# Attention of a two-layer hybrid block: order of the transposes and value products on TensorE, and another spread of the softmax normalisers

## The chip, the cores and the metric

The kernel runs on one core of a Trainium2 chip. Its time is the device time of one execution in microseconds. The core's engines are TensorE (PE in the profile; its weight loads are a row of their own, PEld), VectorE (DVE), ScalarE (ACT), GpSimd (POOL) and SyncE (SP), which issues most of the DMAs. Each engine works through its own queue in order.

## The reference

Two layers of a block over 256 context tokens and 1024 latent tokens of width 1024. Each layer normalises and modulates its input, projects it once, and feeds three groups: a bidirectional SSD, attention, and a convolution module; each is gated, the results are concatenated, projected and added. Only the attention concerns the change. It has 8 heads of 64 in two key/value groups of four heads, and looks at all context keys and a band of latent keys, with a sink logit per head:

```python
def window_attention(q, k, v, kc, vc, sink):
    ...
    s_win = einsum('bnqgrd,bnkgd->bngrqk', qb, kw) * scale      # three blocks of 128 keys, |qpos - kpos| <= 128
    s_ctx = einsum('bnqgrd,btgd->bngrqt', qb, kc) * scale       # 256 context keys
    p = softmax(concatenate([sink_col, s_ctx, s_win]))
    out = (einsum('bngrqt,btgd->bnqgrd', p[..., 1:1 + n_ctx], vc)
           + einsum('bngrqk,bnkgd->bnqgrd', p[..., 1 + n_ctx:], vw))
```

In the first layer the two blocks of context queries attend to the context too; in the last layer there are no context queries.

## The kernel before

Each layer runs three sections in turn: the SSD section, the attention section (att_section, line 965), and the output section. Matmuls of the projections are done in three parts (high by high, low by high, high by low, gemm1, line 464) into tiles named pj.

att_section first makes keys, values and rotated queries, then runs core(n) (line 1024) for each block n of 128 queries: ten calls in layer 0 (two of them context blocks), eight in layer 1. Between the calls it lets the generator rest() (line 1226) go on: the remaining gate projections, the second normalisation of the convolution module and its projection. The loop is at lines 1268 to 1275; each core is traced within high_priority(AHEAD) with AHEAD = 4000, two steps of rest() follow each call.

The code is not in the order of execution. The framework simulates the engines, and gives each engine's next place to the instruction of the highest priority that is ready by that simulation; priority is the place in the program, moved forward by high_priority. The resulting order of each engine's queue is fixed before the program runs. A tile with bufs=2 has two buffers; its third user waits until the first is released.

core(n) has nk key blocks in the list kb: two context blocks, the block itself, and its neighbours where they exist. So nk is 2 for a context block, 4 for the first and the last latent block, 5 for the rest. It works in two halves (for r0 in (0, 2), line 1053) of four heads each:

- Scores of four heads (tiles s5 and s4) with masks added by a matmul with the negated identity; row minimum on VectorE (lines 1064, 1076), Exp with the row sum on ScalarE (lines 1079, 1081) into a tile p of queries by keys. p has six buffers, four of them used by one half.
- For each key block i (line 1083): four transposes (line 1086), one a head, into one PSUM tile pt (two buffers); a copy into the SBUF tile ptt (two buffers), on ScalarE for even i and on VectorE for odd i (lines 1088 to 1091); and two value products (line 1093), one a key/value group. Each has 64 columns of stationary values, 256 columns moving, and adds into its half of the 128 partitions of the PSUM tile op (named o in the rows), which has one buffer.

Behind both halves the normalisers are made: sums with the sink term, and the reciprocal (lines 1095 to 1100), a column per head with a query per partition. They are spread along the free axis by eight matmuls (line 1105) into the tile rb (a buffer of pt): the column, broadcast to 64 columns, as the stationary operand, and the identity moving. A copy to rs on ScalarE (line 1107) and a product on VectorE (line 1108) write the result over the queries, which releases op for the next core.

All matmuls made by the helper mm carry its line, L96, and are told apart by tile names.

Of the kernel before, what the change touches and what calls it, by code (L numbers as in the profile page):

```python
# [2 lines left out]

# [7 lines left out]
F32 = mybir.dt.float32  # L11
# [3 lines left out]
AF = mybir.ActivationFunctionType  # L15
# [4 lines left out]
P = 128  # L20
# [41 lines left out]
RX0 = 6  # L62
NH = 3
NAG = (2, 4)
SEP = (4, 2, 2, 2, 9)


def build(tc, A, out, stop=None, dbg=None):
    nc = tc.nc
# [19 lines left out]
    def f32(ap):  # L89
        return ap.bitcast(F32)  # L90
# [2 lines left out]
        return ap.bitcast(F32R)  # L93

    def mm(o, l, r, start=True, stop=True):
        nc.tensor.matmul(o, l, r, start=start, stop=stop)  # L96

    def spread(o, col):

# [2 lines left out]
    def flat(ap):  # L102
        return ap.rearrange("p a b -> p (a b)")


    ident = cp.tile([P, P], F32, name="ident")
# [155 lines left out]
    with ExitStack() as st:  # L262
# [3 lines left out]
        def tr():  # L266
            return ipp.tile([P, 512], F32, tag="tr", name="tr", bufs=3)
# [22 lines left out]
        pt = tr()  # L290
# [250 lines left out]
    def ssd_section(l, last, early):  # L541
        v1 = vec1[l]
        gblocks = LATB if last else ALLB
        with ExitStack() as st:
# [248 lines left out]
            def gate_gemm(r):  # L793

                w = load_w(l, ((C_AG + r * 64, 64), (C_AG + 256 + r * 64, 64)))

                def use(off, n, ps):
                    t = sp.tile([P, 512], F32, tag="sz", name="ag", bufs=3)[:, 0:n]
                    nc.scalar.activation(out=t, in_=ps, func=AF.Copy)
                    nc.scalar.dma_start(out=agd[l][:, r, off:off + n], in_=t)  # L800
                for blk in gblocks:
                    gemm(l, w, (blk,), use)
# [147 lines left out]
            for i in range(4):  # L950
# [6 lines left out]
                if i == 1:  # L957
                    bc_group(1)
            for r in range(NAG[l]):
                gate_gemm(r)  # L960
# [4 lines left out]
    def att_section(l, last):  # L965
# [5 lines left out]
        with ExitStack() as st:  # L971
# [7 lines left out]
            vtok = sa.tile([P, NCH, P], F32, name="vtok")  # L979
# [42 lines left out]
            sp = pool(f"atc{l}", 1, None, st)  # L1022

            def core(n):
                if n < 2:
                    kb = [0, 1]
                else:
                    kb = [0, 1] + ([n - 1] if n > 2 else []) + [n] + ([n + 1] if n < NCH - 1 else [])
                mpos = [i for i, b in enumerate(kb) if b >= 2 and b != n]
                runs = []  # L1030
                for i, b in enumerate(kb):
                    if runs and runs[-1][0] + runs[-1][2] == b and i < 4:
                        runs[-1][2] += 1
                    else:
                        runs.append([b, i, 1])
                nk = len(kb)
                nb_ = slice(n * P, (n + 1) * P)
                Q = []
                for g in range(2):
                    a, b = slice(g * 64, g * 64 + 64), slice(64 - g * 64, 128 - g * 64)  # L1040
                    t = sp.tile([P, 4, P], F32R, tag="Q", name="Q", bufs=3)
                    nc.scalar.activation(out=t[a], in_=qt[a, :, nb_], func=AF.Copy)
                    nc.vector.tensor_tensor(out=t[b], in0=qt[a, :, nb_], in1=f32(t[a]), op=ALU.subtract)
                    Q.append(t)
                sums = sp.tile([P, 5, 8], F32, tag="sums", name="sums", bufs=2)
                nm, sm_, ns = (sums[:, i, :] for i in range(3))
                op = pp.tile([P, 512], F32, tag="o", name="o")

                def scores(o, g, r, b, cnt, fin, first=True):
                    for ki, K in enumerate((KH[g], KL[g])):  # L1050
                        mm(o, Q[g][:, r, :], K[:, b * P:(b + cnt) * P], start=(first and ki == 0), stop=(fin and ki == 1))

                for r0 in (0, 2):
                    heads = [(g, r) for g in range(2) for r in (r0, r0 + 1)]
                    pr = []

                    if nk > 4:
                        s5 = pp.tile([P, 4, P], F32, tag="s5", name="s5")

                        mm(s5, nident, mask_gt.unsqueeze(1).to_broadcast([P, 4, P]), stop=False)  # L1060
                        for q, (g, r) in enumerate(heads):
                            scores(s5[:, q, :], g, r, kb[4], 1, q == 3, first=False)
                        m5 = sp.tile([P, 4], F32, tag="m5", name="m5", bufs=2)
                        nc.vector.tensor_reduce(out=m5, in_=s5, axis=mybir.AxisListType.X, op=ALU.min)
                    for q, (g, r) in enumerate(heads):
                        s4 = pp.tile([P, 4, P], F32, tag="s4", name="s4", bufs=2)
                        for b, i, cnt in runs:
                            if i < 4:
                                scores(flat(s4[:, i:i + cnt, :]), g, r, b, cnt, not any(x in range(i, i + cnt) for x in mpos))
                        for i in mpos:  # L1070
                            if i < 4:
                                mm(s4[:, i, :], nident, mask_lt if kb[i] < n else mask_gt, start=False, stop=True)
                        s = flat(s4[:, 0:min(nk, 4), :])
                        j = g * 4 + r
                        mx = sp.tile([P, 1], F32, tag="mx", name="mx", bufs=3)
                        nc.vector.tensor_reduce(out=mx, in_=s, axis=mybir.AxisListType.X, op=ALU.min)  # L1076
                        nc.vector.scalar_tensor_tensor(out=nm[:, j:j + 1], in0=mx, scalar=nsink[l][:, j:j + 1], in1=m5[:, q:q + 1] if nk > 4 else mx, op0=ALU.min, op1=ALU.min)  # L1077
                        p = sp.tile([P, 5, P], F32, tag="p", name="p", bufs=6)
                        nc.scalar.activation(out=flat(p[:, 0:min(nk, 4), :]), in_=s, func=AF.Exp, scale=-1.0, bias=nm[:, j:j + 1], accum_out=sums[:, 3, j:j + 1])  # L1079
                        if nk > 4:  # L1080
                            nc.scalar.activation(out=p[:, 4, :], in_=s5[:, q, :], func=AF.Exp, scale=-1.0, bias=nm[:, j:j + 1], accum_out=sums[:, 4, j:j + 1])
                        pr.append(p)
                    for i, b in enumerate(kb):
                        pt = pp.tile([P, 512], F32, tag="pt", name="pt", bufs=2)
                        for q in range(4):
                            nc.tensor.transpose(pt[:, q * P:(q + 1) * P], pr[q][:, i, :], ident)  # L1086
                        ptt = sp.tile([P, 512], F32, tag="ptt", name="ptt", bufs=2)
                        if i % 2:
                            nc.vector.tensor_copy(out=ptt, in_=pt)
                        else:  # L1090
                            nc.scalar.activation(out=ptt, in_=pt, func=AF.Copy)
                        for g in range(2):
                            mm(op[g * 64:(g + 1) * 64, r0 * P:(r0 + 2) * P], vtok[:, b, g * 64:(g + 1) * 64], ptt[:, g * 256:(g + 1) * 256], start=(i == 0), stop=(i == nk - 1))

                nc.vector.tensor_tensor(out=ns, in0=nm, in1=nsink[l], op=ALU.subtract)
                nc.scalar.activation(out=ns, in_=ns, func=AF.Exp)
                nc.vector.tensor_tensor(out=sm_, in0=sums[:, 3, :], in1=ns, op=ALU.add)
                if nk > 4:
                    nc.vector.tensor_tensor(out=sm_, in0=sums[:, 4, :], in1=sm_, op=ALU.add)
                nc.vector.reciprocal(out=sm_, in_=sm_)  # L1100
                rb = pp.tile([P, 512], F32, tag="pt", name="rb", bufs=2)
                for r in range(4):
                    for g in range(2):
                        j = g * 4 + r
                        mm(rb[g * 64:(g + 1) * 64, r * P:(r + 1) * P], sm_[:, j:j + 1].to_broadcast([P, 64]), ident)
                rs = sp.tile([P, 512], F32, tag="ptt", name="rs", bufs=2)
                nc.scalar.activation(out=rs, in_=rb, func=AF.Copy)
                nc.vector.tensor_tensor(out=qt[:, :, nb_], in0=op.rearrange("p (a b) -> p a b", b=P), in1=rs.rearrange("p (a b) -> p a b", b=P), op=ALU.mult)
# [117 lines left out]
            def rest():  # L1226

                def units():
                    rs = list(range(NAG[l], 4))
                    for J in range(8):  # L1230
# [6 lines left out]
                for off, n in qblocks:  # L1237
                    us = sp.tile([P, 4, 512], F32, tag="us", name="us")[:, :, 0:n]
                    for _, k in zip(conv_norm(off, n, us), SEP):
                        for _ in range(k):  # L1240
# [229 lines left out]
```

## Time and profile before

| | us |
|---|---|
| median of 3 runs | 2414.48 (2412.67 to 2416.03) |
| profiled execution, its own time | 2409.47 |
| span of the profiled execution | 2407.7 |
| TensorE busy | 2307.0 (96%), 13453 matmuls |
| VectorE busy | 1533.2 (64%) |
| GpSimd busy | 1085.7 (45%) |
| ScalarE busy | 979.0 (41%), 2123 instructions |

The attention cores of layer 0 run from about 690 to 1040 us of the span, those of layer 1 from about 1875 to 2203. Matmuls overlap: the length of one in the trace goes on past the start of the next, so their distance from start to start tells what they cost. A value product is two entries (passes) in the trace, as is a matmul of the normaliser spread; a transpose and a projection matmul are one. The timeline merges entries of one kind that follow each other, with their number behind the x.

### The profile page before, as it was taken

To read this page: it belongs to the slowest core of one execution; us is meant where nothing else is said; L and a number is where in the kernel's file an instruction comes from. 1 tells how busy PE (TensorE), PEld (TensorE's weight loads), DVE (VectorE), ACT (ScalarE), POOL (GpSimd) and SP (SyncE) were. 2 spreads that over 40 slices of the span, in tenths; PEclk is the share of its full clock that TensorE was granted. 3 is DMA by queue.
4 is the path that set the end of the run, shared out by engine and by line. 5 is a ranking of instruction groups with operands and counts; after the bars stand their busy time and mean duration, and the time that the engine had idled before them with its cause. 6 is when DMAs were issued, how large, how long until landed. Compare 5 with 4: busy or idle time off the path is not lost.

```text
span 2407.7 us, 37133 instructions
## 1 busy us (share of the span) xinstructions
PE 2307.0 (96%) x13453; PEld 1817.5 (75%) x13453; DVE 1533.2 (64%) x2738; ACT 979.0 (41%) x2123; POOL 1085.7 (45%) x1249
## 2 busy tenths in 40 slices
PE   6999999999999999999999999999999999999998
PEld 3787678777877776776888788768768676776798
DVE  4679899941276855865354679979423864865634
ACT  6543243422235454444243443343322355463433
POOL 3237663764453222343233337667575531332333
PEclk8999999999999999999999999999999999999999
DMA  7412212233133112248465311111212312235663
GB/s 225 154 58 87 87 49 64 85 100 111 36 90 105 62 38 70 80 141 264 136 185 168 92 40 45 41 41 43 78 54 62 106 48 67 80 97 171 197 179 107
DMA packets 324248, 237.07 MB, mean 98 GB/s; under 512 B 56066, under 2 KB 280546, under 8 KB 324064
## 3 DMA queue, kind: packets, MB, share of 16 engines
q1 hardware_dynamic: 280832, 193.28, 27.2%
q10 hardware_dynamic: 42336, 41.06, 5.5%
q8 instruction: 106, 1.74, 0.3%
q0 software_dynamic: 896, 0.35, 0.1%
q14 instruction: 78, 0.64, 0.1%
HBM read 181.63 MB, written 53.00 MB: 97 GB/s over the span
## 4 chain that ended last, share of the span: by engine, by line
PE 77%; DVE 9%; DMA 5%; POOL 3%; issue 2%; ACT 2%; SPq 1%; ACTq 0%; DVEq 0%; POOLq 0%
PE pj L96 53%; PE sm L96 6%; PE s L96 4%; PE o L96 3%; PE pt L1086 3%; PE po L96 2%; DVE us L508 2%; DMA raw<-oT 1%; PE pc L96 1%; PE pm L96 1%; DMA wm<-w_mod 1%; POOL ex L893 1%; PE rb L96 1%; DVE acc L596 1%; PE sm L912 1%
## 5 line engine op out<-in xcount | busy, mean ns | idle before, releaser
L96 PE MATMUL pj<-hh,wh 128*128 128x512 f32 (+1 forms) x1840 | 692.7, 377 | 7.8 <-ACT wh L416 2.3
L96 PE MATMUL pj<-hl,wh 128*128 128x512 f32 (+1 forms) x1840 | 686.5, 373 | 1.7 <-POOL hl L199 1.7
L96 PE MATMUL pj<-hh,wl 128*128 128x512 f32 (+1 forms) x1840 | 686.4, 373 | 1.7 <-POOL wl L418 1.6
L418 POOL TENSOR_TENSOR wl<-wr,wh 128x512 fp32r<-128x512 f32 x268 | 362.1, 1354 | 516.8 <-ACT wh L416 482.1
L96 PEld LDWEIGHTS pj<-hh,wh 128*128 128x128 f32 x1840 | 350.0, 190 | 70.7 <-issue 6.8
L96 PEld LDWEIGHTS pj<-hh,wl 128*128 128x128 f32 x1840 | 349.5, 190 | 61.3 <-issue 5.0
L96 PEld LDWEIGHTS pj<-hl,wh 128*128 128x128 f32 x1840 | 350.2, 190 | 59.3 <-issue 5.7
L416 ACT ACTIVATE wh<-wr 128x512 fp32r<-128x512 f32 x344 | 215.6, 630 | 365.5 <-PE pj L96 280.2
L508 DVE SCALAR_TENSOR_TENSOR ua<-gl,vec,ua 128x512 f32<-128x512 f32 (+1 forms) x435 | 303.5, 698 | 12.3 <-ACT ua L506 5.7
L596 DVE SCALAR_TENSOR_TENSOR acc<-raw,vec,acc 128x514 f32<-128x514 f32 (+2 forms) x280 | 191.0, 695 | 21.9 <-ACT acc L593 20.3
L96 PE MATMUL pj<-ho,wh 128*128 128x256 f32 (+1 forms) x896 | 180.3, 300 | 1.0 <-ACT wh L416 1.0
L96 PE MATMUL pj<-hx,wh 128*128 128x512 f32 x512 | 163.7, 400 | 6.9 <-DVE hx L500 2.9
L96 PEld LDWEIGHTS pj<-ho,wh 128*128 128x128 f32 x896 | 145.2, 193 | 6.4 <-ACT wh L416 1.2
L893 POOL TENSOR_TENSOR ex<-ex,eb 64x256 f32<-64x256 f32 x144 | 115.5, 802 | 59.4 <-ACT eb L891 52.4
L933 POOL TENSOR_TENSOR xs<-xk,ws 128x256 f32<-128x256 f32 x144 | 90.7, 641 | 112.0 <-PE sm L96 96.8
L1079 ACT ACTIVATE p<-s,sums 128x512 f32<-128x512 f32 (+1 forms) x144 | 95.5, 663 | 107.7 <-DVE sums L1077 69.4
L1076 DVE TENSOR_REDUCE mx<-s 128x1 f32<-128x512 f32 (+1 forms) x144 | 92.4, 654 | 72.0 <-PE s L96 71.6
L96 PE MATMUL pj<-ho,wl 128*128 128x256 f32 (+1 forms) x448 | 134.6, 301 | 1.1 <-POOL wl L418 0.8
L508 DVE SCALAR_TENSOR_TENSOR us<-gl,vec,us 128x512 f32<-128x512 f32 (+1 forms) x150 | 130.3, 869 | 6.8 <-ACT us L506 4.3
L96 PEld LDWEIGHTS pj<-hx,wh 128*128 128x128 f32 x512 | 97.8, 192 | 30.6 <-DVE hx L500 4.7
L907 POOL TENSOR_TENSOR yp<-yp,ye 128x256 f32<-128x256 f32 x136 | 104.3, 783 | 26.6 <-DVE ye L906 26.1
L1086 PE MATMUL pt<-ident,p 128*128 128x128 f32 x640 | 108.5, 283 | 7.2 <-ACT p L1079 6.5
(325 smaller groups left out, 3951.6 us busy)
## 6 DMA issues: line engine op xcount, KB each, us to landing
wr<-w_in SPq DMA_DIRECT2D x160, 256.0 KB
wr<-w_out SPq DMA_DIRECT2D x114, 256.0 KB
wm<-w_mod SPq DMA_DIRECT2D x64, 256.0 KB
raw<-oT ACTq DMA_DIRECT2D x64, 256.0 KB
wr<-w_out SPq DMA_DIRECT2D x76, 128.0 KB
yT<-yT ACTq DMA_DIRECT2D x72, 128.0 KB
wm<-w_mod SPq DMA_DIRECT2D x16, 512.0 KB
wr<-w_in SPq DMA_DIRECT2D x64, 128.0 KB
```

What stands on the lines that cost most here:

```text
L96: nc.tensor.matmul(o, l, r, start=start, stop=stop)
L416: nc.scalar.activation(out=hi, in_=raw, func=AF.Copy)
L418: low_eng[0].tensor_tensor(out=lo, in0=raw, in1=f32(hi), op=ALU.subtract)
L508: nc.vector.scalar_tensor_tensor(out=u if t == 30 else acc, in0=g[:, t:t + n], scalar=vec2[l][:, t, j:j + 1], in1=acc, op0=ALU.mult, op1=A ...
L596: nc.vector.scalar_tensor_tensor(out=acc, in0=raw[:, i0 + t:i0 + t + n], scalar=v1[:, cw:cw + 1], in1=acc, op0=ALU.mult, op1=ALU.add)
L893: nc.gpsimd.tensor_tensor(out=e[q, :, q], in0=e[q, :, q], in1=eb[q], op=ALU.add)
L907: nc.gpsimd.tensor_tensor(out=y, in0=y, in1=ye, op=ALU.add)
L912: nc.tensor.matmul(ps[:, jj * P:(jj + 1) * P], y[:, jj * P:(jj + 1) * P], ident, start=(jj == 0), stop=False, is_transpose=True)
L933: nc.gpsimd.tensor_tensor(out=h3(xs), in0=xc(c), in1=hb(ws3, c, d), op=ALU.mult)
L1076: nc.vector.tensor_reduce(out=mx, in_=s, axis=mybir.AxisListType.X, op=ALU.min)
L1079: nc.scalar.activation(out=flat(p[:, 0:min(nk, 4), :]), in_=s, func=AF.Exp, scale=-1.0, bias=nm[:, j:j + 1], accum_out=sums[:, 3, j:j + 1])
L1086: nc.tensor.transpose(pt[:, q * P:(q + 1) * P], pr[q][:, i, :], ident)
```

## The change

Inside a half, the loop over key blocks is split. The transposes and the copy of one block become the function turn(i). Blocks 0 and 1 are turned first. Then, for each pair of blocks, the next two blocks are turned, with a priority 40 places further forward, and behind them the value products of the pair are traced within issue_after, which makes each TensorE instruction in it stand behind the last transpose in TensorE's queue. Where a pair has no further block to turn, the last transpose is that of an earlier turn.

The normalisers are first copied by ScalarE into a tile nx (which takes one of the six p buffers): 128 queries by four blocks of 128, each of the two halves of a block holding one head's normaliser 64 times. Four whole transposes of these blocks into rb take the place of the eight matmuls.

```diff
+TURN = 40
 ...
+        return nc.tensor.matmul(o, l, r, start=start, stop=stop)
+
+    def after(ins):
+        return tc.issue_after(ins[0].ins) if ins else nullcontext()
 ...
-                    for i, b in enumerate(kb):
+                    ptts, last_t = [], []
+
+                    def turn(i):
                         pt = pp.tile([P, 512], F32, tag="pt", name="pt", bufs=2)
                         for q in range(4):
-                            nc.tensor.transpose(pt[:, q * P:(q + 1) * P], pr[q][:, i, :], ident)
+                            last_t[:] = [nc.tensor.transpose(pt[:, q * P:(q + 1) * P], pr[q][:, i, :], ident)]
                         ptt = sp.tile([P, 512], F32, tag="ptt", name="ptt", bufs=2)
                         if i % 2:
                             nc.vector.tensor_copy(out=ptt, in_=pt)
                         else:
                             nc.scalar.activation(out=ptt, in_=pt, func=AF.Copy)
-                        for g in range(2):
-                            mm(op[g * 64:(g + 1) * 64, r0 * P:(r0 + 2) * P], vtok[:, b, g * 64:(g + 1) * 64], ptt[:, g * 256:(g + 1) * 256], start=(i == 0), stop=(i == nk - 1))
+                        ptts.append(ptt)
+                    for i in range(min(nk, 2)):
+                        turn(i)
+                    for i0 in range(0, nk, 2):
+                        with tc.high_priority(TURN):
+                            for i in range(i0 + 2, min(nk, i0 + 4)):
+                                turn(i)
+                        with after(last_t):
+                            for i in range(i0, min(nk, i0 + 2)):
+                                for g in range(2):
+                                    mm(op[g * 64:(g + 1) * 64, r0 * P:(r0 + 2) * P], vtok[:, kb[i], g * 64:(g + 1) * 64], ptts[i][:, g * 256:(g + 1) * 256], start=(i == 0), stop=(i == nk - 1))
 ...
                 rb = pp.tile([P, 512], F32, tag="pt", name="rb", bufs=2)
+
+                nx = sp.tile([P, 5, P], F32, tag="p", name="nx", bufs=6)
+                nc.scalar.activation(out=nx[:, 0:4, :].rearrange("p r (g q) -> p r g q", g=2), in_=sm_.rearrange("p (g r) -> p r g", g=2).unsqueeze(3).to_broadcast([P, 4, 2, 64]), func=AF.Copy)
                 for r in range(4):
-                    for g in range(2):
-                        j = g * 4 + r
-                        mm(rb[g * 64:(g + 1) * 64, r * P:(r + 1) * P], sm_[:, j:j + 1].to_broadcast([P, 64]), ident)
+                    nc.tensor.transpose(rb[:, r * P:(r + 1) * P], nx[:, r, :], ident)
```

## Rows read from the trace of the kernel before

**Rows 1.** The page: busy time, share and instructions; the chain's shares by engine.
```profile
PE 2307.0 (96%) x13453; PEld 1817.5 (75%) x13453; DVE 1533.2 (64%) x2738; ACT 979.0 (41%) x2123; POOL 1085.7 (45%) x1249
...
PE 77%; DVE 9%; DMA 5%; POOL 3%; issue 2%; ACT 2%; SPq 1%; ACTq 0%; DVEq 0%; POOLq 0%
```

**Rows 2.** Windows: stretch, length, busy PE PEld DVE ACT POOL, clock, DMA share, GB/s.
```profile
690.00:1050.00 360.00, 354.12 (x2225) 266.71 (x2224) 240.25 (x465) 175.43 (x460) 114.31 (x91) 1.00 0.26 76
1875.00:2215.00 340.00, 326.55 (x1870) 233.04 (x1869) 229.44 (x414) 168.62 (x417) 114.56 (x81) 0.99 0.29 90
690.00:720.00 30.00, 25.27 (x139) 19.77 (x138) 29.14 (x56) 12.49 (x33) 13.60 (x11) 0.94 0.32 96
...
1875.00:1950.00 75.00, 68.20 (x355) 49.12 (x353) 62.84 (x91) 35.52 (x81) 41.15 (x28) 1.00 0.30 94
...
2130.00:2190.00 60.00, 56.85 (x334) 40.56 (x333) 35.85 (x83) 30.67 (x69) 14.73 (x11) 1.00 0.27 86
```

**Rows 3.** Waits of PE, 1875 to 2215: us in total, times, longest.
```profile
PE o L96 <- DVE ptt L1089: 2.1, 3, 1.0
```

**Rows 4.** Tile o: duration ns min/median/max, first and last start, forms.
```profile
L96 PE MATMUL o<-ptt,vtok x640: 379/379/689, 705.9 to 2195.1; 128*64 128x256 f32 x160
```

**Rows 5.** Tile rb, all calls.
```profile
L96 PE MATMUL rb<-ident,sums x288: 272/273/323, 724.1 to 2195.9; 128*64 128x128 f32 x144
L1107 ACT ACTIVATE rs<-rb x18: 578/598/628, 725.2 to 2199.0; 128x512 f32<-128x512 f32 x18
```

**Rows 6.** Timeline of PE, 2095.8 to 2098.7.
```profile
2095.83 0.39 PE L96 MATMUL pj<-hh,wh 128*128 128x512 f32 x1
2096.06 1.04 PE L1086 MATMUL pt<-ident,p 128*128 128x128 f32 x8
2096.85 0.47 PE L96 MATMUL pj<-hl,wh 128*128 128x512 f32 x1
2097.16 0.39 PE L96 MATMUL pj<-hh,wl 128*128 128x512 f32 x1
2097.39 0.40 PE L96 MATMUL pj<-hh,wh 128*128 128x512 f32 x1
2097.72 0.65 PE L96 MATMUL o<-ptt,vtok 128*64 128x256 f32 x4
2098.30 0.50 PE L96 MATMUL pj<-hl,wh 128*128 128x512 f32 x1
2098.64 0.39 PE L96 MATMUL pj<-hh,wl 128*128 128x512 f32 x1
```

**Rows 7.** Timeline of PE, 2109 to 2111.2: start, length, line, out<-in, form, number.
```profile
2109.06 0.39 PE L96 MATMUL pj<-hh,wl 128*128 128x512 f32 x1
2109.38 1.08 PE L96 MATMUL o<-ptt,vtok 128*64 128x256 f32 x8
2110.39 0.66 PE L1086 MATMUL pt<-ident,p 128*128 128x128 f32 x4
2110.80 0.47 PE L96 MATMUL pj<-hh,wh 128*128 128x512 f32 x1
2111.11 0.39 PE L96 MATMUL pj<-hl,wh 128*128 128x512 f32 x1
```

**Rows 8.** Timeline of PE: a whole spread in one run.
```profile
2159.78 1.09 PE L96 MATMUL rb<-ident,sums 128*64 128x128 f32 x16
```

**Rows 9.** Timeline of PE: the first and the last group of 154.
```profile
705.92 1.08 PE L96 MATMUL o<-ptt,vtok 128*64 128x256 f32 x8
...
2195.18 1.04 PE L96 MATMUL rb<-ident,sums 128*64 128x128 f32 x14
```

**Rows 10.** Timeline of DVE: a copy of an odd block.
```profile
2057.80 0.68 DVE L1089 COPY ptt<-pt 128x512 f32<-128x512 f32 x1
```

**Rows 11.** Timeline, 742 to 746: reciprocal and spread of the second core.
```profile
742.87 0.20 DVE L1100 RECIPROCAL sums<-sums 128x8 f32<-128x8 f32 x1
...
745.10 1.04 PE L96 MATMUL rb<-ident,sums 128*64 128x128 f32 x16
```

More of the change, by code (lines that the diff above doesn't have):

```diff
@@ L1 @@
-from contextlib import ExitStack
+from contextlib import ExitStack, nullcontext
 from itertools import chain
@@ L95, in mm @@
     def mm(o, l, r, start=True, stop=True):
-        nc.tensor.matmul(o, l, r, start=start, stop=stop)
+        return nc.tensor.matmul(o, l, r, start=start, stop=stop)
+    def after(ins):
+        return tc.issue_after(ins[0].ins) if ins else nullcontext()
     def spread(o, col):
```

## The prediction

> **What bounds the kernel now.** I began with the page: TensorE is busy 96% of the span, none of the other engines over 64%, and the chain of waits runs 77% through TensorE and 9% through VectorE [rows 1]. Then the windows of the two attention stages, the only places that the diff touches: together 700 us, in which TensorE is busy 680.7, VectorE 469.7, ScalarE 344.1, at a granted clock of 1.00 and 0.99 (the 2.4 GHz level) [rows 2]. Three stretches of them hold most of the idle time: the first 30 us of layer 0's, the first 75 us of layer 1's (there VectorE is busy 62.8 of 75) and 2130 to 2190, together 165 us with 14.7 us of TensorE idle [rows 2]. In the remaining 535 us TensorE has 4.6 us of idle time, and the value products' waits for VectorE's copies of the transposes, which the change reorders, are 2.1 us in three waits in the whole of layer 1's stage [rows 3]. So in three quarters of the stages each microsecond of matmul time is a microsecond of the stage; the reader should look for what a matmul costs there in start-to-start time, not in the busy sums, since neighbouring matmuls overlap.
>
> **What a group of value products costs.** The trace has 640 passes of value products (two for each of 320 products, both halves of the 128 columns running side by side) [rows 4] and 288 of the normaliser spread [rows 5]; all of these use 64 columns of the array (the form 128\*64), everything around them 128. I read the price from starts. Between projections one projection matmul starts 0.23 us after the last, and eight transposes between them take 2095.83 to 2097.16 less two such steps, 0.87, that is 0.109 each with nothing for entering or leaving [rows 6]. The length of a merged row of eight value passes (two blocks) is 1.08, of four 0.65 [rows 6, 7]: the difference, 0.43, is the work of one block. But four passes between projections take 2097.39 to the second projection behind them at 2098.64 less two steps, 0.79 [rows 6], so 0.36 is paid for the group itself: the step into it is 0.33 for 0.23, and the step behind it and the one after are long too. Eight passes with four transposes behind them take 2109.06 to 2111.11 less two steps and 0.44 of transposes, 1.15 [rows 7], of which 0.86 is work and 0.29 the group, although it is twice as long. I take 0.35 a group, nearest to the row with nothing but projections around it, and treat groups of the spread alike; their 16 passes are 16 x 0.0545 = 0.87 of work ((1.09 - 0.27)/15, by the row's length and one pass's [rows 5, 8]). In the timeline of TensorE the value products form 146 rows and the spread 36; where such rows touch they are one group, which leaves 154 groups, 84 in layer 0's stage and 70 in layer 1's, the first and the last of them in [rows 9].
>
> **The change part by part.**
> (1) Value products in pairs. There are 36 half cores (18 calls of core, two halves): 24 with five key blocks, 8 with four, 4 with two. With every pair whole they make 24 x 3 + 8 x 2 + 4 x 1 = 92 groups; with no pair whole, 160. The new order pins the products behind the transposes of the blocks after next, but not to each other: the first pair of a half finds both its copies done, because the transposes ahead of it needed the buffers that these copies free; the second pair has no such guarantee, its second copy (on VectorE, 0.68 us [rows 10] and whatever is queued there) may come after the first product was issued. I take half of the second pairs (24 + 8) as split: 92 + 16 = 108. Groups saved: 154 - 108 = 46, at 0.35 that is 16.1 us. Bounds: 62 groups, 21.7 us; or six more than now, 2.1 us lost.
> (2) The spread. 288 passes at 0.0545, 15.7 us, go; 18 x 4 transposes at 0.109, 7.8 us, come; 7.9 us saved. Its groups of their own vanish in the count of (1), since the transposes need none. Here the trace is to be held against the Trainium skill, "TensorEngine Tiling (Array Packing)", section Theoretical Speedup: a matmul with 64 columns or fewer gains up to 2x by running in two tiles at once, which speaks for keeping the spread as it was. If that halved its 8 products to four slots of 0.109, the old work would cost 0.44 a core, as much as four whole transposes, and only the 16.1 of (1) would be left. The row says 0.87 a core: the halves do run side by side, but each product is two passes.
> (3) The new ScalarE copy of the normalisers, 18 times 512 elements. The trace doesn't show it; the nearest rows are the copy rs of the same size, 0.60 [rows 5], and an engine half idle (175.4 and 168.6 busy of 360 and 340 [rows 2]). What hides it is the time between the reciprocal and the spread, 2.0 us in the shortest of the 18 cases [rows 11]. I take nothing; if it were exposed in each core 18 x 0.6 = 11 us. It also takes one of six probability buffers for the while; a following Exp that waits costs the path nothing as long as TensorE has projections to run, and at most the same 11 us.
> (4) Transposes earlier. Four transposes and one copy (ScalarE for even blocks, VectorE for odd) of each later block gain 40 places of priority; they can now pass Exps, reductions and convolution steps on these two queues; no DMA and nothing on SP's or POOL's is moved. Their number is unchanged, so their cost is nothing, by the cover of (1).
> (5) The added wait. Value products stand in TensorE's queue behind the last transposes, which wait for a copy of VectorE to free their buffer. Projections and the scores of the next half are what else the queue holds; whoever is put behind a waiting transpose waits as well. There are 24 x 2 + 8 = 56 such places. Below: 0, or a gain of the few us of waits that there are now. Above: one copy, 0.68 us each [rows 10], 38 us. I take 0, nearest to the row of waits [rows 3].
>
> **Sum.** 16.1 + 7.9 = 24.0 us of TensorE time. In 165 of the 700 us the stage hangs on other engines too [rows 2]; there I count nothing as gained: 24.0 x 535/700 = 18.3. The profiled execution took 2409.47 for a span of 2407.7 and would take 2391.2; the median of the runs is 5.0 us above it, and 2414.5 - 18.3 = 2396.
>
> **Rivals.**
> *All of it arrives*: 92 groups and no loss in the three stretches: 21.7 + 7.9 = 29.6, 2385. For it: most idle time there is at the beginning of a stage, where few products run. Against: the VectorE copies of the second pairs.
> *The pairs don't form* (the change doesn't do what it says): the copies come one by one, products are issued one block at a time as before, 160 groups: 7.9 - 2.1 = 5.8, of which 4.4 arrives, 2410. For it: today the two buffers would allow the order in which two blocks' products run together, and it is found in a minority of the groups.
> *The cores' own chain sets the pace*: scores, reduction, Exp, copies and normaliser of 18 cores, with projections only as filling. Then TensorE's saving turns into idle time once the projections are used up, 2414 give or take 4. For it: the last spread of layer 1 stands at 2195.18 [rows 9], 20 us before that stage ends, so cores and projections run out nearly together. Against: no idle time of TensorE in 535 us.
> *Stalls at the pairs (slower)*: mechanism (5). The place is the transposes of the third and fourth block; the price a VectorE copy, 0.68 us plus a convolution step ahead of it. From 24/56 = 0.43 us of mean stall on, the gain is gone; at 0.68 in all 56 the kernel is 38 - 24 = 14 us slower, 2428. For it: VectorE is busy two thirds of the stages. Against: [rows 3].
>
> **Chances.** Forecast (2389 to 2404) 0.52, all of it 0.15, pairs don't form 0.08, the cores' chain 0.11, stalls 0.14. The range 2383 to 2417 takes in the first two, the two without effect and the beginning of the stalls. Differences under 0.2% (4.8 us) can't be told from none: faster 0.70 (the first two and the edge of the third), within 0.2% 0.16, slower 0.14.
>
> **What would show it.** Right: TensorE has 13453 - 288 + 72 = 13237 matmuls and ScalarE 18 instructions more; no form 128\*64 but the value products, in about 108 groups (92 to 125), most of eight passes, four only at the end of a half; transposes in runs of eight; the two attention stages 16 to 20 us shorter in sum and everything else as long as before; waits of TensorE for ptt still under 5 us a stage. Wrong if the number of groups is above 140 (1), if idle time of TensorE in the stages grows by over 10 us (the cores' chain, at the end of a stage; stalls, behind DVE ptt at the pairs), if the spread's transposes wait for the new copy (3), or if the time moves outside the attention stages.

## The result, and the profile after

The median of the changed kernel is 2392.22 us (2390.28 to 2399.68, 4 runs), beside 2413.57 for the kernel before (2412.64 to 2416.03, 4 runs): a ratio of 0.9918, 95% interval 0.9905 to 0.9931, so 17 to 23 us less. The forecast was 2396. The profiled execution took 2391.2 us for a span of 2389.5, 18.2 less than the one before. Of the runs below, e10 had two and e11 one execution in a slower state (2835 to 9854 us), which count in their medians and not in the ratios; without them the medians are 2419.80 and 2405.77.

The page of the changed kernel, busy times and the chain by engine, beside [rows 1]:

```profile
PE 2286.8 (96%) x13237; PEld 1813.4 (76%) x13237; DVE 1528.7 (64%) x2738; ACT 990.3 (41%) x2141; POOL 1074.5 (45%) x1249
...
PE 77%; DVE 9%; DMA 6%; ACT 2%; POOL 2%; issue 2%; SPq 1%; ACTq 0%; DVEq 0%; POOLq 0%
```

TensorE's busy time is 20.2 us lower and its idle time (span less busy) 2.0 higher. Its 13237 matmuls and ScalarE's 18 more instructions are those of the forecast.

To see where the time went I cut both spans at the same four events: the first key tile of each layer's attention, the first write of the residual xb in layer 0's output section, and the first gated tile hx of layer 1's. Windows of the kernel before (columns as in [rows 2]): attention of layer 0, then its output section and the SSD of layer 1, attention of layer 1, the last output section.

```profile
596.70:1117.60 520.90, 508.21 (x2938) 389.74 (x2937) 314.46 (x591) 229.59 (x558) 190.88 (x149) 0.99 0.30 90
1117.60:1807.80 690.20, 665.62 (x3656) 543.51 (x3654) 442.04 (x730) 253.93 (x492) 351.65 (x458) 0.99 0.31 90
1807.80:2200.50 392.70, 382.75 (x2137) 281.71 (x2137) 238.31 (x439) 176.57 (x431) 147.33 (x106) 1.00 0.26 80
2200.50:2407.70 207.20, 194.10 (x1246) 174.97 (x1244) 110.28 (x177) 80.36 (x138) 76.11 (x60) 0.97 0.56 171
```

The same four of the changed kernel:

```profile
594.80:1104.80 510.00, 499.36 (x2824) 389.58 (x2823) 314.94 (x595) 236.91 (x570) 189.23 (x149) 0.98 0.31 93
1104.80:1792.20 687.40, 664.44 (x3649) 542.17 (x3647) 436.51 (x726) 254.00 (x490) 346.09 (x458) 0.99 0.31 90
1792.20:2180.70 388.50, 374.83 (x2041) 279.33 (x2041) 242.31 (x441) 181.95 (x439) 145.46 (x107) 1.00 0.27 82
2180.70:2389.50 208.80, 194.74 (x1244) 175.94 (x1244) 103.70 (x174) 79.87 (x138) 74.68 (x60) 0.97 0.56 166
```

The attention sections are 10.9 and 4.2 us shorter, 15.1 together. The other 3.1 us are outside what the diff touches: 1.9 ahead of the first cut, 2.8 between the layers, and 1.6 given back at the end. In the two sections TensorE is busy 16.8 us less and idle 1.7 us more (22.6 before, 24.3 after).

The tiles that the change touches, in the kernel after (columns as in [rows 4]; ScalarE's new copy, the spread, the value products):

```profile
L1121 ACT ACTIVATE nx<-sums x18: 614/630/632, 719.1 to 2174.8; 128x512 f32<-128x512 f32 x18
...
L1123 PE MATMUL rb<-ident,nx x72: 270/273/477, 723.9 to 2178.4; 128*128 128x128 f32 x72
...
L97 PE MATMUL o<-ptt,vtok x640: 378/380/690, 704.0 to 2178.8; 128*64 128x256 f32 x160
```

Two places of its TensorE timeline show the new order and the prices:

```profile
903.51 0.39 PE L97 MATMUL pj<-hh,wl 128*128 128x512 f32 x1
903.74 0.60 PE L1094 MATMUL pt<-ident,p 128*128 128x128 f32 x4
904.27 1.08 PE L97 MATMUL o<-ptt,vtok 128*64 128x256 f32 x8
905.28 0.66 PE L1123 MATMUL rb<-ident,nx 128*128 128x128 f32 x4
905.77 3.60 PE L97 MATMUL po<-us,pw 128*128 128x512 f32 x8
...
948.75 0.40 PE L97 MATMUL pj<-hl,wh 128*128 128x512 f32 x1
949.07 0.65 PE L97 MATMUL o<-ptt,vtok 128*64 128x256 f32 x4
949.66 0.66 PE L1123 MATMUL rb<-ident,nx 128*128 128x128 f32 x4
950.07 0.48 PE L97 MATMUL pj<-hh,wl 128*128 128x512 f32 x1
950.39 0.39 PE L97 MATMUL pj<-hh,wh 128*128 128x512 f32 x1
```

In the first, 903.51 to 905.77 less one projection step (0.23) and eight transposes (0.87) leaves 1.16 for eight value passes, whose work is 0.86: the group costs 0.30. In the second, 948.75 to 950.39 less two projection steps, four transposes and four passes leaves 0.31. Over all groups the step into one is 0.095 longer than its work and the steps out of it 0.20 (medians), 0.295 together. There are 105 groups, 54 and 51 by layer: 53 of eight passes, two of twelve, 40 of four, ten of two or six passes. Before there were 154.

So the work taken from TensorE is by this estimate 49 x 0.295 + 7.85 for the spread = 22.3 us, and the profiled execution is 18.2 us shorter.

### The profile page after: what moved, and what is told of

The parts are those of the page before. It is cut to its first block, busy times and chain, and to the rows that moved or that the text cites. A ratio compares the mean times of both kernels' runs of the same rounds, so it can differ in the third digit from the quotient of the medians.

```text
span 2389.5 us, 36713 instructions
## 1 busy us (share of the span) xinstructions
PE 2286.8 (96%) x13237; PEld 1813.4 (76%) x13237; DVE 1528.7 (64%) x2738; ACT 990.3 (41%) x2141; POOL 1074.5 (45%) x1249
## 4 chain that ended last, share of the span: by engine, by line
PE 77%; DVE 9%; DMA 6%; ACT 2%; POOL 2%; issue 2%; SPq 1%; ACTq 0%; DVEq 0%; POOLq 0%
PE pj L97 54%; PE sm L97 6%; PE s L97 4%; PE o L97 3%; PE pt L1094 3%; DVE us L513 3%; PE po L97 2%; DMA raw<-oT 2%; PE pc L97 1%; PE pm L97 1%; DMA wr<-w_out 1%; DMA wm<-w_mod 1%; PE sm L917 1%; DVE acc L601 1%; SPq L292 1%
## 5 line engine op out<-in xcount | busy, mean ns | idle before, releaser
L97 PE MATMUL pj<-hh,wh 128*128 128x512 f32 (+1 forms) x1840 | 693.9, 378 | 11.4 <-DVE kb L999 3.3
L97 PEld LDWEIGHTS pj<-hh,wh 128*128 128x128 f32 x1840 | 350.3, 190 | 80.6 <-issue 10.6
L601 DVE SCALAR_TENSOR_TENSOR acc<-raw,vec,acc 128x514 f32<-128x514 f32 (+2 forms) x280 | 190.4, 692 | 24.2 <-ACT acc L598 22.6
L97 PE MATMUL pj<-hx,wh 128*128 128x512 f32 x512 | 166.3, 406 | 10.5 <-DVE hx L505 4.8
```

The costliest lines, as they stand in the source:

```text
L97: return nc.tensor.matmul(o, l, r, start=start, stop=stop)
L601: nc.vector.scalar_tensor_tensor(out=acc, in0=raw[:, i0 + t:i0 + t + n], scalar=v1[:, cw:cw + 1], in1=acc, op0=ALU.mult, op1=ALU.add)
```

## The experiments

All ran beside the kernel before, whose medians were 2412.96 (e1 to e4), 2412.3 (e5 to e8) and 2412.32 (e9 to e12). First the results of those that were timed; "work" is the change of TensorE time worked out as above (0.295 a group, 7.85 for the new spread). The next three columns compare the profiled execution with that of before: TensorE busy, TensorE idle, and the time lost where the granted clock was 0.50 (half the length of those stretches; 35.5 us before). Busy and idle add up to the change of the span; the half clock is part of both, and where idle time falls into it, it is counted in both columns (counting it once makes the half-clock entries up to 3.2 us smaller, e11's the most). Each row rests on one trace; after and e9, the same kernel, differ by 3.7 us of idle time and 1.5 of half clock. The profiled execution of e6 took 6.9 us more than its median, those of e5, e11 and the rest are within 3.7 of theirs.

| | groups | work | busy | idle | half clock | median | ratio (95%) |
|---|---|---|---|---|---|---|---|
| after | 105 | -22.3 | -20.2 | +2.0 | +0.5 | 2392.22 | 0.9918 (0.9905, 0.9931) |
| e1 pairs only | 108 | -13.6 | -9.3 | +3.9 | +2.2 | 2405.55 | 0.9967 (0.9956, 0.9978) |
| e2 spread only | 144 | -10.8 | -5.4 | +8.8 | +6.2 | 2415.41 | 1.0008 (0.9998, 1.0018) |
| e3 no pin | 130 | -14.9 | -14.3 | +0.9 | -2.5 | 2396.57 | 0.9930 (0.9917, 0.9943) |
| e4 triples | 84 | -28.5 | -23.0 | +5.4 | +7.8 | 2391.64 | 0.9907 (0.9892, 0.9922) |
| e5 late copy | 93 | -25.8 | -14.2 | +11.0 | +10.5 | 2403.97 | 0.9970 (0.9961, 0.9979) |
| e6 spread, late copy | 131 | -14.6 | -10.1 | +16.2 | +8.7 | 2408.71 | 0.9990 (0.9981, 0.9999) |
| e7 triples, late copy | 77 | -30.6 | -24.0 | +18.6 | +9.6 | 2403.46 | 0.9963 (0.9951, 0.9976) |
| e9 after, again | 105 | -22.3 | -20.1 | +5.7 | +2.0 | 2394.96 | 0.9923 (0.9909, 0.9937) |
| e10 before, other order | 146 | -2.4 | +3.0 | +5.8 | +6.2 | 2420.06 | 1.0030 (1.0019, 1.0041) |
| e11 after, other order | 104 | -22.6 | -11.8 | +12.2 | +12.0 | 2406.11 | 0.9969 (0.9954, 0.9983) |
| e12 triples, one DVE copy | 87 | -27.6 | -26.3 | +2.9 | 0.0 | 2387.41 | 0.9896 (0.9881, 0.9912) |

**The two parts alone.** e1 is the kernel after with the old spread:

```diff
-                nx = sp.tile([P, 5, P], F32, tag="p", name="nx", bufs=6)
-                nc.scalar.activation(out=nx[:, 0:4, :]...)
                 for r in range(4):
-                    nc.tensor.transpose(rb[:, r * P:(r + 1) * P], nx[:, r, :], ident)
+                    for g in range(2):
+                        j = g * 4 + r
+                        mm(rb[g * 64:(g + 1) * 64, r * P:(r + 1) * P], sm_[:, j:j + 1].to_broadcast([P, 64]), ident)
```

> The changed loop over key blocks with the old spread of the normalisers. Its TensorE queue has 108 groups of 64-column matmuls (the changed kernel 105, the kernel before 154), as the old spread mostly stands beside value products. Group theory (0.35 us a group, 7.9 us of work of the old spread, about four fifths arriving): 7 us over the changed kernel, 2399. Rival, the spread's part was nothing because the new ScalarE copy and longer way cost what the matmuls saved: 2392, as the changed kernel.

e2 is the kernel before with the reverse of these lines, the new spread in its old loop.

> The kernel before with the new spread alone. 144 groups. Group theory: 7.9 + 10 x 0.35 = 11.4 us of TensorE time, four fifths of it arriving, 9 us under the kernel before, 2404 to 2405. Rival, the added ScalarE copy lengthens the way from reciprocal to result and holds the next core: no faster than before, 2411 to 2414. If the two parts add up, this gain and the distance of e1 from the kernel before together give the whole change.

Measured: e1 is 7.4 us faster than before; e2 is 2.5 us slower, which its interval does not tell from no change. The two parts do not add up to the 21 of both. Group theory had 2399 and 2404 to 2405; e2 lies just above its rival's 2411 to 2414. The groups are as counted (108 and 144), and in e2 the spread's work is gone from TensorE, but it does not arrive. e2's attention sections:

```profile
594.80:1119.20 524.40, 506.95 (x2822) 386.61 (x2822) 315.69 (x595) 237.81 (x570) 192.35 (x149) 0.98 0.30 91
1809.20:2204.20 395.00, 381.37 (x2041) 279.20 (x2041) 242.57 (x441) 182.51 (x440) 146.48 (x107) 0.98 0.26 80
```

TensorE is idle 31.1 us of them, 8.4 more than before, and the clock is 0.98 in layer 1 where it was 1.00. Idle time and half clock together, +15.0 over the whole kernel (13.9 with the overlap counted once), are larger than the saving of 10.8.

**The pin.** e3 takes out the order of products behind transposes; the queue is left to the planner.

```diff
-                        with after(last_t):
+                        with nullcontext():
```

> The changed kernel without the pin: transposes still run two blocks ahead with the raised priority, but value products may be queued when ready. 130 groups instead of 105. Group theory: 25 x 0.35 = 8.6 us more TensorE time, four fifths arriving, 2399. Rival (the gain comes from transposes running ahead, so that products no longer wait for copies, and not from the number of groups): as the changed kernel, 2390 to 2394.

It has 130 groups and is 4.35 us slower than the changed kernel by medians, between its two expectations, where 25 groups at 0.295 make 7.4. The time alone does not settle it: the two intervals overlap, and e9, the changed kernel again, is 2.7 us slower than its first measurement. The counts do: the pin is worth 25 of the 49 groups; of the other 24, ten go with the new spread alone (e2).

**Three blocks.** e4 queues three blocks' products in a run, with a third ptt buffer, taken from p's six; the normaliser blocks nx move from a p buffer to a ptt buffer (not shown).

```diff
-                    for i in range(min(nk, 2)):
-                        turn(i)
-                    for i0 in range(0, nk, 2):
+                    for i in range(min(nk, 3)):
+                        with tc.high_priority(TURN if i > 1 else 0):
+                            turn(i)
+                    for i0 in range(0, nk, 3):
 ...
-                            for i in range(i0 + 2, min(nk, i0 + 4)):
+                            for i in range(i0 + 3, min(nk, i0 + 3 + 2)):
 ...
-                            for i in range(i0, min(nk, i0 + 2)):
+                            for i in range(i0, min(nk, i0 + 3)):
```

> Products of three blocks in one run behind the transposes of the next two: three ptt buffers, five p buffers instead of six, the normaliser blocks in a ptt buffer. 84 groups instead of 105. Group theory: 21 x 0.35 = 7.3 us less TensorE time, 5 to 6 arriving, 2386 to 2387. Rival (the cores' own chain sets the pace by now; the longer wait for three copies and the buffer less for Exp cost more): 2392 or more, with more idle time of TensorE in the attention stages.

It has 84 groups, 6 us less work than after, and the same time (2391.64, where group theory had 2386 to 2387), with 3.4 us more idle time and 7.3 more of half clock than after. Waits of TensorE for ptt behind the first 580 us of e4:

```profile
PE pt L1094 <- DVE ptt L1097: 9.8, 7, 3.6
...
PE pt L1094 <- ACT ptt L1099: 2.5, 5, 0.7
```

This is the wait that the prediction's step (5) priced: transposes that need the buffer which a VectorE copy frees. It appears here, at 9.8 us in seven places (2.2 in two in the changed kernel).

**Who gets the buffer.** In every kernel with the new spread the cores of layer 0 end later: the last normalised queries of that layer come 442.7 us behind its first key tile before, 444.4 in e1, but 482.7 after and 492.6 in e2. (In layer 1 they do not: 394.0 before, 387.2 after, 393.6 in e2.) My theory was that nx, taking a p buffer at once, holds up the next Exp. e5 to e7 make the copy later, behind the last ScalarE copy of a half.

```diff
+                last_c = []
 ...
-                            nc.scalar.activation(out=ptt, in_=pt, func=AF.Copy)
+                            last_c[:] = [nc.scalar.activation(out=ptt, in_=pt, func=AF.Copy)]
 ...
-                nc.scalar.activation(out=nx[:, 0:4, :]...)
+                with tc.issue_after(last_c[0].ins):
+                    nc.scalar.activation(out=nx[:, 0:4, :]...)
```

> The changed kernel with one more pin: the ScalarE copy that spreads the normalisers into nx stands behind the last ScalarE copy of transposes of the second half, so that nx doesn't take a p buffer while the transposes of that half still hold four of the six. 93 groups (changed kernel 105). Buffer theory (in the changed kernel and in e2 nx holds a p buffer for 5 to 20 us a core, the next core's Exps start later, the cores of layer 0 end 40 to 50 us later and the tail of that section is exposed): the last product of layer 0's cores comes about 445 us after the section's first key as in the kernel before (443) and e1 (444), not 483; with 12 groups x 0.3 less, 2385 to 2388. Rival (the buffer does no harm, the way from reciprocal to result is long in itself): 2389 to 2393, cores ending as late as in the changed kernel.

> The kernel before with the new spread alone, and with the same pin of the nx copy. 131 groups (before 154, e2 144). Buffer theory: now the spread's 7.9 us and 23 x 0.3 = 6.9 us arrive for the most part, 2401 to 2405. Rival (the new spread is worth nothing by itself): 2411 to 2416 as e2.

e7 adds it to e4, with six p buffers and two of Q in place of three.

> Runs of three blocks (three ptt buffers) with all six p buffers, two Q buffers instead of three, and nx pinned late. 77 groups. Group theory: 28 x 0.3 = 8.4 us of TensorE time less than the changed kernel; if it arrives, 2383 to 2385. Rival (the cores' chain with fewer Q buffers is the bound, and e4 showed how idle time takes it back): 2390 or more, with more idle time of TensorE in the attention stages.

The theory fell. In e5 the cores still end at 485.6, and the kernel is 9 to 12 us slower than the changed one (e9, after) although it has twelve groups fewer; 2403.97 lies above both of its expectations. e6 is 7 us faster than e2 by medians, between its two expectations and within what another order of the same instructions moves (below); e7, at 2403.46, leaves TensorE the least work and the most idle time, as its rival had it. Idle time and half clock take back 21.5, 24.9 and 28.2 us (20.8, 24.3 and 26.7 with the overlap counted once). e5's attention sections:

```profile
596.30:1110.00 513.70, 495.31 (x2817) 386.55 (x2816) 321.90 (x595) 235.78 (x570) 187.89 (x149) 0.98 0.30 91
1804.10:2198.80 394.70, 379.96 (x2041) 282.30 (x2041) 246.36 (x441) 180.16 (x440) 146.82 (x107) 0.97 0.26 79
```

**What a group pays for.** If the price is the change between 64 and 128 columns, value products of 128 columns have none. e8 lets both key/value groups' values stand as 128 columns and adds both products into the same region, so that it leaves out the separation of the two groups and what it computes is not the attention:

```diff
-                                    mm(op[g * 64:(g + 1) * 64, r0 * P:(r0 + 2) * P], vtok[:, kb[i], g * 64:(g + 1) * 64], ptts[i][:, g * 256:(g + 1) * 256], ...)
+                                    mm(op[:, r0 * P:(r0 + 2) * P], vtok[:, kb[i], :], ptts[i][:, g * 256:(g + 1) * 256], ...)
```

> The changed kernel with each value product over all 128 columns of values (both key/value groups, added into one region, so half of what is added is not the attention's). No instruction of 64 columns is left in the attention; the two products of a block no longer run side by side, so a block's work doubles, 160 x 0.43 = 69 us more. Form theory (the price of a group is the change between 64 and 128 columns): the 105 x 0.3 = 31 us of group prices go, the step into and out of a run of products is as between projections, and the kernel takes about 2392 + 38 = 2430. Rival (the price belongs to two-pass products following one-pass matmuls, whatever their width): the long steps stay, 2455 to 2461.

One execution took 2441.36 us, between form theory's 2430 and the rival's 2455 to 2461. Its attention sections are 41.0 us longer than those of the kernel after, where twice the products' work less 105 group prices makes 160 x 0.43 - 31 = 38; the other 9 us of its span lie outside of these sections, where nothing was changed. The timeline of TensorE in e8:

```profile
947.08 0.60 PE L1094 MATMUL pt<-ident,p 128*128 128x128 f32 x4
947.51 1.89 PE L97 MATMUL o<-ptt,vtok 128*128 128x256 f32 x8
949.24 0.60 PE L1123 MATMUL rb<-ident,nx 128*128 128x128 f32 x4
949.60 0.48 PE L97 MATMUL pj<-hh,wh 128*128 128x512 f32 x1
```

Four transposes into products take 0.43 = 4 x 0.109, with nothing added (0.53 in the kernel after, same sequence); eight passes into transposes 1.73 = 8 x 0.216, nothing added either. The two-pass products are still there and the long steps are not, so it is the change of form that costs; and the two 64-column halves do run side by side: 0.108 a pass against 0.216. The Trainium skill, "TensorEngine Tiling (Array Packing)", section Key Properties, says that changing the tiling mode drains TensorE; these rows agree with it, at 0.30 for the way in and out.

**How much the order alone is worth.** e9 is the changed kernel again. e10 and e11 are the kernels before and after with three steps of rest() behind every core in place of two: the same instructions, another order in the fixed queues.

```diff
-FLN = (2, 2)
+FLN = (3, 3)
```

> The changed kernel itself once more, for its median on this chip and for a second trace of it. If idle time in the sections is a property of the fixed queues, the second trace repeats the first's: TensorE idle 10 to 12 us in layer 0's attention, 13 to 15 in layer 1's, time 2390 to 2394. If it is chance of the execution, the idle time moves by several us and the median with it.

> Control: the kernel before with three steps of the other work traced behind each core instead of two (FLN 3, 3). All instructions are the same, only the order of the queues moves (146 groups instead of 154, 2.4 us less TensorE time). If an order is worth only its TensorE work: 2409 to 2412. If the ends of the sections weigh as much as the groups, as e1, e2 and e5 suggest: anywhere within 8 us of the kernel before, in either direction, with idle time of TensorE to match.

> The changed kernel with the same other pace (FLN 3, 3); 104 groups. By TensorE work 42 groups x 0.3 + 7.9 = 20.5 us under e10, about 2391; the share that arrives there against e10 tells whether the four fifths of the change itself hold for another order. If the interplay decides: between 2384 and 2404.

e9 repeats the result (0.9923), 1 us above its range, with 11.1 us of idle time in layer 0's attention and 11.4 in layer 1's, where 13 to 15 were expected. The other order costs 7.7 us in the kernel before and 11 to 14 in the one after, as much as the parts of the change are worth, while the change itself is worth 14.0 us in that order (2420.06 to 2406.11), of 20.2 us of work. So e10 moved as its second expectation allowed, and e11 lies above both of its own. In layer 1's attention e11 loses 13.5 us to the half clock, the kernel after 1.5. Windows of e11 around one such fall:

```profile
2095.00:2101.00 6.00, 5.55 (x37) 4.09 (x35) 3.97 (x7) 5.16 (x12) 3.14 (x3) 1.00 0.36 105
2101.40:2118.50 17.10, 14.66 (x66) 12.25 (x68) 10.45 (x25) 8.45 (x21) 9.12 (x8) 0.50 0.34 109
2118.50:2130.00 11.50, 10.18 (x63) 7.72 (x60) 9.99 (x33) 9.47 (x22) 1.75 (x2) 1.00 0.37 112
```

and its timeline of TensorE there:

```profile
2099.67 1.02 PE L97 MATMUL pz<-ones,acc 128*128 128x1 f32 x8
2103.84 0.69 PE L1094 MATMUL pt<-ident,p 128*128 128x128 f32 x2 [3.15 <-ACT p L1084]
```

TensorE ran at the 2.4 GHz level, waited 3.15 us for one Exp, and from 2101.4, within this wait, had the 1.2 GHz level for 17.1 us, which takes up to 7.3 us (half of the 14.66 in which it was busy) beside the 3.15 of the wait. Windows of e5:

```profile
2080.00:2094.00 14.00, 11.58 (x80) 8.12 (x79) 13.84 (x19) 11.02 (x27) 9.78 (x8) 1.00 0.40 114
2094.00:2104.20 10.20, 10.01 (x46) 7.97 (x46) 7.44 (x28) 2.81 (x9) 2.55 (x2) 0.50 0.30 103
```

Here idle time of 2.4 us in a stretch of 14 is followed by 10.2 us at 0.50 though TensorE is busy in 10.0 of them. A wait does not always bring it: the kernel after keeps 1.00 over a stretch with 1.9 us of idle time in ten.

```profile
2095.00:2105.00 10.00, 8.06 (x59) 5.21 (x59) 9.76 (x37) 7.43 (x23) 2.54 (x2) 1.00 0.35 113
```

**A better version.** e12 is e4 with only the second block's copy on VectorE; the fourth goes to ScalarE.

```diff
-                        if i % 2:
+                        if i == 1:
```

> As e4 (runs of three blocks, 5 p buffers, normaliser blocks in a ptt buffer), but of the five copies of a half only that of block 1 on VectorE, the others on ScalarE. 87 groups. e4 lost 9.8 us of TensorE time to transposes that waited for VectorE's copies, behind its reductions and convolution steps. If those waits are what took e4's gain: 2383 to 2387, with TensorE's waits for VectorE's copies under 3 us. Rival (ScalarE's queue, Exps and weight copies, is no better): 2390 to 2396, the waits on ScalarE's copies instead.

2387.41 us, the lowest median of all, 7.6 below e9, which ran beside it, and 4.2 below e4, whose interval overlaps its own. Its waits for ptt, beside those of e4:

```profile
PE pt L1094 <- DVE ptt L1097: 4.0, 5, 1.2
PE pt L1094 <- ACT ptt L1099: 4.0, 6, 1.5
```

VectorE's fall from 9.8 to 4.0 us (under 3 was expected), ScalarE's rise from 2.5 to 4.0, and the half clock is back at the 35.5 us of before, 7.8 less than in e4. Which of the two made the time is not separated.

## Why the prediction was right

The forecast of 2396 lies 4 us above the result, and each step can be held against rows. Of the signs named beforehand, the numbers of matmuls and instructions, the range of groups and the small growth of idle time came true. Others did not: the two sections are 15.1 us shorter, just under the 16 to 20; transposes stand in a run of eight 17 times, against 15 before; groups of four do not stand only at the end of a half.

**(1) Groups.** 105 against 108 forecast, from 154 by the same count. The nearness is in part luck. Of the 32 second pairs, of which half were taken as split, seven are; but four first pairs and two single last blocks are split too, which the forecast held whole: 92 + 7 + 4 + 2. The price was mis-sized: 0.35 was read at a group of four with projections around it, most groups have transposes on a side, and the medians give 0.295. So 49 groups gave 14.5 us, not 16.1. What it is paid for was open then; e8 shows it.

**(2) Spread.** 72 transposes in place of 288 passes; four take 0.41 us from start to start in nine of the 18 spreads, and 0.35 to 0.59 where else they stand whole at the full clock; a whole old spread took 0.87 of work [rows 8] and the entry and exit of a group. The 7.9 stands as a term of TensorE's time. The halves of the old spread did run side by side, as those of the value products do against e8, and that is contained in its 0.87. The Trainium skill, "TensorEngine Tiling (Array Packing)", section Theoretical Speedup, gives up to 2x for two tiles; e8's rows agree with that.

**(3) The new copy** is 0.63 us long, 18 times, starts 0.0 to 0.8 us behind the reciprocal, and its transposes come 4 to 20 us later, and no wait of TensorE names it: hidden, as forecast.

**(4) and (5) Earlier transposes and the added wait.** Waits of TensorE in layer 1's attention before, beside [rows 3]:

```profile
PE pt L1086 <- ACT ptt L1091: 0.8, 1, 0.8
PE o L96 <- ACT ptt L1091: 0.5, 1, 0.5
```

and after:

```profile
PE pt L1094 <- ACT p L1084: 2.9, 3, 2.3
PE pt L1094 <- ACT ptt L1099: 2.4, 4, 1.2
PE pt L1094 <- DVE ptt L1097: 2.2, 2, 1.2
...
PE o L97 <- ACT ptt L1099: 0.7, 2, 0.3
```

For ptt that is 5.3 us in layer 1 (0.2 in layer 0), a little over the 5 allowed (3.8 in e9), from 3.4 and 1.1 before: about 1 us more in all, not the 38 of the rival "stalls at the pairs". The rival's mechanism is real: at three blocks a run the waits for ptt ahead of transposes are 12.3 us (e4).

**The share that arrives.** I took 535/700, on the ground that in three stretches the stage hangs on other engines. 18.2 of 22.3 (82%) arrived in the profiled pair; by the medians of the two measurements the kernel gains 21.4 and 17.4. The number was near by luck: the reason is not what the runs show. Were a quarter lost to other engines, TensorE's idle time would have grown by 5.7 us (24.0 x 165/700), and it grew by 1.7 in both sections, not at all in e9. What varies is what the new order does to waits and clock: in the attention of layer 0 the half clock took 5.1 us more than before (11.9 against 6.8 in its first 510 us). With -22.3 of work, +4.9 of clock in both sections and +1.7 idle the sum for the sections is -15.7; measured -15.1. The two sections of e9 repeat it: 4.9 us more of half clock than before, 22.5 idle, and 16.0 us shorter.

```profile
595.40:1105.40 510.00, 498.88 (x2825) 388.19 (x2824) 317.06 (x595) 237.29 (x571) 190.58 (x149) 0.98 0.30 91
1796.50:2184.10 387.60, 376.20 (x2041) 280.11 (x2041) 242.19 (x441) 182.11 (x439) 146.21 (x107) 0.99 0.27 82
```

Over the whole kernels e2, e5 and e11 the same two items took 15 to 24 us. In the table work and half clock together give the change of TensorE's busy time within 4.2 us in all twelve rows, within 2.3 in nine.

**Everything else as long as before** was not quite so. Ahead of the first cut the half clock took 8.5 us where it took 11.9 in the profile of before, and 10.2 in e9: it differs between executions of unchanged code. Between the layers e9 took 691.1 us, not less than the 690.2 of before, so the 2.8 gained there are no effect of the change that repeats. The tail of layer 0's attention, inside the first section, moved too. Waits of TensorE there, before (1000 to 1118):

```profile
PE po L96 <- DVE acc L1217: 3.4, 2, 2.6
PE po L96 <- DVE sgl L1209: 1.2, 2, 0.7
```

and after (990 to 1105):

```profile
PE pj L97 <- DVE hx L505: 2.0, 1, 2.0
PE pj L97 <- ACT hx L504: 0.9, 1, 0.9
```

The convolution's waits went, those of the next projection came, with a net gain of some 1.7 us (the same waits in e9) that no step of mine contained.

**The cores' own chain**, a rival, is half there: the cores of layer 0 end 40 us later behind the section's start, and in all runs with the new spread 26 to 50 us later. In the kernel after enough projections are left to hide it (layer 0's section has 10.6 us of idle time, 12.7 before). Why the new spread does it stays open: moving the copy (e5 to e7) did not change it, nor did a ptt buffer for nx among other changes (e4 481.9, e12 483.5), and I tried no other buffer with everything else as it was. The longer way from the reciprocal to the result, e5's rival, was not tested alone; in the first two cores it is 6.4 and 8.9 us, where it was 5.0 and 5.1. Open too is which part of e2's loss is this and which the order as such.

## What to carry to other kernels

On a TensorE that is nearly always busy, count changes between narrow and full stationary forms, not instructions: each run of 64-column products cost 0.30 us here however long it was, and each run that is saved by queuing more products together takes that much off TensorE's work. But with fixed queues any edit also reorders everything behind it, and the same instructions in another order moved this kernel by 8 to 14 us: read idle time and granted clock beside busy time, and try a change in a second order before a part of it is called useless or good. When runs get longer, look for the buffer whose copy is on the busier engine; moving one copy a half to ScalarE gave the lowest median (2387.41), 4 us below the run without it, though that difference is not clear of noise.

## What the runs showed of the hardware that was not expected

- A run of fp32 products of the form 128\*64 between work of the form 128\*128 costs 0.095 us on the way in and 0.20 on the way out; with 128\*128 throughout both vanish (e8).
- Two 64-column products side by side pass in half the time of two full-width ones: 0.108 against 0.216 us a pass of 256 columns.
- Around a wait of 3.15 us (e11) and behind 2.4 us of idle time in 14 (e5) the granted clock fell to 0.50, for 17.1 and 10.2 us, though TensorE was busy again for most of it (14.66 and 10.01 us). Over a kernel half the length of such stretches is 33 to 48 us, the idle time in them included; between two orders of the same work (after and e11) it differs by 11.5.
